# Where a decoder trunk forms the query and key weights of its attention units 8, 9 and 10

## The chip, the cores and the metric

The kernel runs on one core of one Trainium2 chip, in one launch. The metric is the device time of an execution in microseconds; less is better. Times are medians of several runs.

## The reference

The reference is a decoder trunk of two layers over 1024 positions of width 1024, all in 32-bit floats. Each layer has a token mixer and then a dense MLP with a squared ReLU; each of these is preceded by an RMS norm and added to the residual, and a final RMS norm ends the trunk.

```python
for layer in range(DEPTH):                      # DEPTH = 2
    y = _rms_norm(h, mix_norm_g[layer])
    if layer % 2 == 0: y = _chunk_gating_mixer(y, ...)      # spatial gating MLP, chunks of 128
    else:              y = _dilated_attention_mixer(y, w_qkv, w_out, rel_bias)
    h = h + y
    y = _rms_norm(h, mlp_norm_g[layer])
    h = h + jnp.square(jax.nn.relu(y @ w_up[layer])) @ w_down[layer]
return _rms_norm(h, final_norm_g)
```

The mixer of layer 0 is a gating MLP. That of layer 1 is a causal attention with 8 heads of 64 in each of three dilation groups (1, 4 and 16), whose outputs are merged by their softmax denominators. The MLPs go from 1024 to 4096 and back.

## The kernel before, in words

**Numbers.** TensorE multiplies in a reduced format (fp32r). To keep the accuracy of 32-bit floats, each operand is split into an upper and a lower half (hi and lo), and a product is three matmuls: hi by hi, hi by lo, lo by hi. Function `split` (L219 to L221) does this: ScalarE copies the source to hi (L220), and an engine, mostly VectorE, subtracts hi from the source to give lo (L221). Nearly all tiles are 128 by 512.

**Products by seven.** The large products are formed by a scheme of Strassen's kind: of a 2 by 2 block product, seven products (numbered 1 to 7) of sums and differences of blocks are computed instead of eight. So each weight comes as four blocks, from which seven operands are formed by a few additions and seven splits.

**Order of the phases.** Gating mixer of layer 0, up and down projection of the first MLP, values of the attention, the attention's 12 units, output projection, and the second MLP. A unit is a pair of heads in one dilation group; `unit_qk` computes its queries and keys with seven products from the weights `wd[i, p]` of unit `i`. Scores, softmax, transposes and products with the values of earlier units are woven between these products by a planner (`Flow`), which counts TensorE's time while the program is written and lets generators go on when their due time has come. The order of TensorE is thereby fixed in the program; the order of the other engines follows the program and the dependencies, each engine's queue being in order.

**Weights formed ahead.** The seven operands of a unit's weights are formed ahead of time and saved in DRAM (`wd`): loaded blocks are added, subtracted, split, and hi and lo are stored. In the attention they are only loaded again (`unit_weights`, tile wp, L1241), seven loads of 512 KB for a unit. Before the change they are formed in these places:
- units 1 to 6 in the gating mixer, by `prepare`;
- unit 11 (`APART`) in the up projection of the first MLP, by `prepare_apart`, after other weights;
- unit 7 among the values of the attention, by `attended`;
- units 8, 9 and 10 in the attention itself, by `attended` with a pace of 7000 ns a part, from 12 us after the first unit's start on.

`prepare_apart(i)` is a generator of eight parts for a unit. All eight together issue 6 loads of 256 KB, 4 additions or subtractions on VectorE (L584 to L600) and 7 splits. `placed` puts the 14 stores of the halves on a list (`unsaved`), and `save` issues what is on the list on SP's queue (L556); it is called after a later step, so that a store doesn't wait for its split at the head of the queue. The attention's version keeps its tiles apart from the others: loaded blocks and lower halves in the ring r (4 tiles, name ra), upper halves in the ring b (2 tiles, name hi), which the attention's bias tiles use as well. The other places take all tiles from the ring t (13 tiles, names t and tr).

**The down projection** (`Down.run`) has 18 steps, `t` = 0 to 17. A step forms one block column of the output with seven products of up to four k-blocks, in the order 1, 5, 7, 6, 2, 3, 4; with four k-blocks a product has 12 matmuls. After each product, VectorE empties the bank into h (L1067) or into a sum (L1099); after product 1, ScalarE copies it. Behind that, for each product, `then` calls `more()`, which forms one of the seven weights wp of the next step (GpSimd makes the sums, L376 to L381, ScalarE and VectorE split), and `inputs`, which loads one hidden tile (t from hid) and splits it into hx for the next step. Banks `d` and `e` hold products 5 and 7 and, emptied, products 3 and 4. In the last steps fewer k-blocks are left, the products are shorter, and the last inputs (xe) are loaded. Then `close` ends the layer and the first tiles of the attention begin.

Of the kernel before, what the change touches and what calls it, by code (L numbers as in the profile page):

```python
# [12 lines left out]
F32 = mybir.dt.float32  # L13
F32R = mybir.dt.float32r
# [5 lines left out]
P = 128  # L20
D = 1024
S = 1024
HALF = 512
# [8 lines left out]
def half(s):  # L32
    return slice(s * HALF, (s + 1) * HALF)


def blk(b, n=1):
    return slice(b * P, (b + n) * P)
# [75 lines left out]
LATER = (2, 4, 6)  # L113

CALM = (1600.0, 1600.0, 1200.0, 1600.0)
PREPARED = ((1, 2, 3, 4, 5, 6), (7,), (8, 9, 10))
APART = 11
EARLY = 4
PACE = (1700.0, 1800.0, 3000.0, 7000.0)
LAT = dict(sum=2600.0, rms=2600.0, tile=1600.0, gate=8500.0, soft=5500.0, turn=4200.0, fe=1300.0, v=2000.0, qk=4200.0, merge=2600.0, out=700.0, fex=3.0, ve=1600.0, vd=6000.0, ex=18000.0, ones=900.0)  # L120


# [1 line left out]
def trunk(ctx: ExitStack, tc: tile.TileContext, xT, w_u, w_v, w_o, w_s, b_s, w_qkv, w_vt, w_bo, rel,  # L124
          w_up, w_dn, w_dl, vecs, onehot, outT):
    nc = tc.nc
    flow = Flow()
# [4 lines left out]
    tpool = ctx.enter_context(tc.tile_pool(name="tpool", bufs=13))  # L132
# [3 lines left out]
    dram = ctx.enter_context(tc.tile_pool(name="dram", bufs=2, space=DRAM))  # L136
# [8 lines left out]
    def rtemp():  # L145
        return tpool.tile([P, HALF], F32R, tag="t", name="tr")
# [5 lines left out]
    class Pair:  # L152
# [6 lines left out]
        def split(self, src, engine=None):  # L159
            n = src.shape[1]  # L160
            split(self.hi[:, 0:n], self.lo[:, 0:n], src, engine)
            return self
# [13 lines left out]
    def load(src, t=None):  # L176

        src, n = src if isinstance(src, list) else [src], 0
        t = raw() if t is None else t
        for x in src:  # L180
            nc.sync.dma_start(t[:, n:n + x.shape[1]], x)
            n += x.shape[1]
        return t[:, 0:n]

    def mm_bank():
        return psm.tile([P, HALF], F32, tag="mm", name="mm")
# [157 lines left out]
    SEVEN = (1, 5, 7, 6, 2, 3, 4)  # L344
# [155 lines left out]
        flow.add((terms.second if s else terms.first)(sq, gi), LAT["sum"])  # L500


    wd = {(i, p): dram.tile([P, 2, HALF], F32, name=f"wd{i}_{p}", bufs=1) for i in (*sum(PREPARED, ()), APART) for p in SEVEN}

    def prepare(unit_list, pace):

# [32 lines left out]
    LATE_DL = {("dl", 1, a): w_dl[1, a] for a in range(4)}  # L539
    wl = {key: dram.tile([P, 2, HALF], F32, name="wl" + "_".join(map(str, key)), bufs=1) for key in (*LATE, *LATE_DL)}  # L540

    def fetch(src, own=rtemp):
        r = own()
        return r, load(src, r.bitcast(F32))

    def apart():
        return tpool.tile([P, HALF], F32R, tag="r", name="ra", bufs=4)

    def above():
        return tpool.tile([P, HALF], F32R, tag="b", name="hi", bufs=2)  # L550

    unsaved = []

    def save():
        for dst, t in unsaved:
            nc.sync.dma_start(dst, t.bitcast(F32))  # L556
        unsaved.clear()

    def placed(dst, held, own=rtemp):
        lo, r = held  # L560
        hi = own()
        split(hi, lo, r)
        unsaved.extend((dst[:, e, :], t) for e, t in enumerate((hi, lo)))

    def prepare_late(src):

        keys = list(src)
        held = fetch(src[keys[0]])
        yield
        for n, key in enumerate(keys):  # L570
            last, held = held, fetch(src[keys[n + 1]]) if n + 1 < len(keys) else None
            placed(wl[key], last)
            yield

    def prepare_apart(i, own=rtemp, upper=rtemp):

        tt = nc.vector.tensor_tensor
        n = 3 * (i // 3 * 3 + ORDER[i % 3])
        src = lambda a, b: w_qkv[n + a][:, half(b)]
        get = lambda a, b: fetch(src(a, b), own)  # L580
        put = lambda p, held: placed(wd[i, p], held, upper)
        r10, r11 = get(1, 0), get(1, 1)
        yield
        tt(r10[1], r10[1], r11[1], op=ALU.add)  # L584
        r00 = get(0, 0)
        put(4, r11)
        yield
        x = own()
        x = x, x.bitcast(F32)
        tt(x[1], r10[1], r00[1], op=ALU.subtract)  # L590
        put(5, r10)
        yield
        r11 = get(1, 1)
        put(1, r00)
        yield
        tt(r11[1], r11[1], x[1], op=ALU.subtract)
        r01 = get(0, 1)
        put(7, r11)
        yield
        tt(r01[1], r01[1], x[1], op=ALU.subtract)  # L600
        again = get(0, 1)
        put(3, r01)
        yield
        put(6, x)
        yield
        put(2, again)
        yield

    def attended(unit_list, pace, *own):
        for i in unit_list:  # L610
            for _ in prepare_apart(i, *own):
                yield pace
                save()
        save()

    coming_late = [chain(prepare_late(LATE), prepare_apart(APART)), prepare_late(LATE_DL)]

    def late(*key, place=None):
        w = (place or wpair)()
        nc.sync.dma_start(w.t.bitcast(F32), wl[key])  # L620
        return w
# [106 lines left out]
    for gi, chunks in enumerate(((0, 1, 2), (3, 4, 5), (6, 7))):  # L728
        banks = {}
        for k in range(KT):  # L730
# [29 lines left out]
            for e, i, n, f in order:  # L760
                x, c = ys[n // 4][k], blk(n % 4)
# [31 lines left out]
    for tiles in ((0, 1, 2), (3,), (4,), (5, 6, 7)):  # L793
        w = [weight(w_u[m]) for m in tiles]
        if tiles[0] == 3:
            flow.add(prepare(PREPARED[0], PACE[0]))
        for s in range(2):
            for i, m in enumerate(tiles):
                b = mm_bank()
# [9 lines left out]
    for tiles in ((0, 1), (2,), (3,), (4, 5, 6, 7)):  # L809
        w = [weight(w_o[m]) for m in tiles]  # L810
        for s in range(2):
            for i, m in enumerate(tiles):
                b = mm_bank()
# [196 lines left out]
    class Down:  # L1010
# [43 lines left out]
        def run(self, w):  # L1054
            for t, (a, ks) in enumerate(self.todo):
                hs = {(i, s): h[a + 4 * i][:, half(s)] for i in range(2) for s in range(2)}
                wn = None
                if t < 17:
                    wn = self.weights(t + 1, **(dict(own=temp, place=pair) if t == 16 else {}))
                more = ahead(wn)  # L1060
                more()

                def xs(p):
                    return [self.x[self.order[k]][p] for k in ks]

                def add(i, s, src, engine=nc.vector):
                    return engine.tensor_tensor(hs[i, s], hs[i, s], src, op=ALU.add).ins  # L1067

                def then(evacuated, p):

                    with tc.issue_after(evacuated) if t < 3 else nullcontext():
                        more()
                        self.inputs(t + 1, (p,))

                if t == 16:
                    self.ends(0)
                a_ = mm_bank()
                product(a_, w[1], xs(1))
                if t < 4:
                    self.u[a] = spare() if t < 2 else temp()  # L1080
                    more()
                    nc.scalar.activation(self.u[a], a_, AF.Copy)
                    self.inputs(t + 1, (1,))
                else:
                    more()
                    sums = mm_bank()
                    nc.scalar.activation(sums, a_, AF.Copy)
                    self.inputs(t + 1, (1,))
                d = at_bank()
                product(d, w[5], xs(5))  # L1090
                then(add(1, 1, d), 5)
                e = at_bank()
                product(e, w[7], xs(7))
                then(add(1, 1, e), 7)
                if t == 16:
                    self.ends(1)
                b = at_bank() if t < 4 else sums
                product(b, w[6], xs(6), t >= 4)
                then(nc.vector.tensor_tensor(self.u[a], self.u[a], b, op=ALU.add).ins, 6)  # L1099
                product(a_, w[2], xs(2), True)  # L1100
                then(add(0, 0, a_), 2)
                product(d, w[3], xs(3), True)
                then(add(0, 1, d), 3)
                if t >= 14:
                    for i, s in ((1, 1), (0, 1)):
                        add(i, s, self.u[a], nc.gpsimd)
                product(e, w[4], xs(4), True)
                self.emptied = add(1, 0, e)
                then(self.emptied, 4)
                if t >= 14:  # L1110
                    add(1, 0, self.u[a], nc.gpsimd)
                w = wn
# [96 lines left out]
    def own(t, g):  # L1209
        return t if g == 0 else t.rearrange("p (q r) -> p q r", r=DIL[g])  # L1210
# [71 lines left out]
    def value_operands():  # L1282
# [3 lines left out]
        fetched = lambda p, k: [load(w_vt[a, b + k], raw() if p == 5 and not b else temp()) for a, b in parts[p]]  # L1286
        total, held = {}, [fetched(*x) for x in order[:EARLY]]
        for n, (p, k) in enumerate(order):
            r = held.pop(0)
            if n + EARLY < len(order):  # L1290
                held.append(fetched(*order[n + EARLY]))
            x = r[0]
# [10 lines left out]
    def all_values():  # L1303

        operands, wv = value_operands(), []
        for s in range(2):
# [13 lines left out]
            for b, bank in enumerate(banks):  # L1320
                value_store(0, 4 * s + b, bank)
        flow.add(terms_a.differences(PACE[1]))

# [8 lines left out]
        for n, p in enumerate(VSEQ):  # L1332
# [6 lines left out]
            if p == 6:  # L1339
                flow.add(attended(PREPARED[1], PACE[2]))  # L1340
            opens = p in (1, 2, 5)
# [440 lines left out]
    all_values()  # L1782
    for gen in (scorer, turner, valuer):
        flow.add(gen())
    flow.add(attended(PREPARED[2], PACE[3], apart, above), 12000.0)
    for i in range(NU):
        unit_qk(i)
    sq = [Square(half(s), (0, 5)) for s in range(2)]
# [127 lines left out]
```

## Time and profile before

| | |
|---|---|
| runs without profile, us | 2141.2, 2147.09, 2149.47 (median 2147.09) |
| profiled execution, us | 2150.69 |
| its span, first to last instruction, us | 2149.0 |
| TensorE busy (matmuls) | 2103.0 us, 98% |
| VectorE busy | 1575.6 us, 73% |
| ScalarE busy | 1183.9 us, 55% |
| GpSimd busy | 498.0 us, 23% |
| mean granted TensorE clock | 0.993 |

In the profile's rows, PE is TensorE (PEld its weight loads), DVE is VectorE, ACT is ScalarE, POOL is GpSimd and SP the engine that issues nearly all DMAs; a q behind a name is the engine's sequencer, L192 a line of the kernel, and out<-in are tiles by their names in the program. Matmuls are pipelined, so that the recorded duration of one is longer than the distance to the next. A row of waits names who waited, the releaser, the total in us, the number of waits and the longest. The chain of waits is followed back from the last instruction to what released it at each point. All window times are us from the start of the span. Weights of units 8 to 10 are formed from 1059.7 to 1281 us of the profiled execution; the steps 6 to 18 of the first down projection lie between 686 and 905 us.

### The profile page before, as it was taken

The page shows a single profiled execution, that of the slowest core. Times are in us where ns is not written, and L with a number is a line of the kernel's source. Part 1 is how long each engine was busy: PE and PEld are TensorE (multiplying, and loading weights), DVE is VectorE, ACT ScalarE, POOL GpSimd, SP SyncE. Part 2 cuts the span into 40 slices and gives each one's busy share as a digit, 9 for nine tenths or more (in the row PEclk, how much of TensorE's full clock was granted, in tenths as well). Part 3 has the DMA queues.
Part 4 walks back from the last instruction along what each step waited for, and adds up shares of the span by engine and source line. Part 5 has one row for each costly group of instructions (what it writes and reads, how often), then busy time and mean ns, then how long its engine had stood idle before and what let it go on. Part 6 is the DMA issues. An engine that isn't in the chain of part 4 may idle for free.

```text
span 2149.0 us, 30646 instructions
## 1 busy us (share of the span) xinstructions
PE 2103.0 (98%) x10144; PEld 1736.4 (81%) x10144; DVE 1575.6 (73%) x2904; ACT 1183.9 (55%) x2384; POOL 498.0 (23%) x370
## 2 busy tenths in 40 slices
PE   8999999999999999999998989999999999999997
PEld 7888888888878888878887778877888888888886
DVE  7878769666689777787666666656985555988776
ACT  7645436566665444346466665666465556544432
POOL 2000224332333332420000000002442332432244
PEclk9999999999999999999999999999999999999998
DMA  6338814587765453445876766481256443654432
GB/s 216 123 92 285 289 55 151 199 274 276 261 202 188 154 160 118 160 174 200 316 217 217 227 202 182 154 266 59 79 201 210 153 157 123 211 162 153 147 113 79
DMA packets 224756, 387.10 MB, mean 180 GB/s; under 512 B 39897, under 2 KB 67668, under 8 KB 224596
## 3 DMA queue, kind: packets, MB, share of 16 engines
q1 hardware_dynamic: 215456, 383.77, 53.8%
q10 hardware_dynamic: 9140, 1.36, 0.4%
q8 instruction: 80, 1.31, 0.3%
q14 instruction: 80, 0.66, 0.1%
HBM read 252.24 MB, written 132.81 MB: 179 GB/s over the span
## 4 chain that ended last, share of the span: by engine, by line
PE 79%; DVE 8%; DMA 6%; ACT 3%; issue 2%; POOL 1%; SPq 1%; ACTq 0%; DVEq 0%; POOLq 0%
PE at L192 40%; PE mm L192 39%; DMA wd<-hi 2%; PE at L199 1%; DMA t<-in_w_qkv 1%; DVE tr L221 1%; DVE t L221 1%; DVE y L221 1%; POOL t L278 1%; DMA r<-in_w_v 1%; ACT t L1496 1%; DVE wp L221 1%; DMA V<-vd 0%; DVE r L438 0%; DVE h L333 0%
## 5 line engine op out<-in xcount | busy, mean ns | idle before, releaser
L221 DVE TENSOR_TENSOR wp<-r,wp 128x512 fp32r<-128x512 f32 (+3 forms) x399 | 322.8, 814 | 138.9 <-ACT wp L220 136.5
L220 ACT ACTIVATE wp<-r 128x512 fp32r<-128x512 f32 (+3 forms) x399 | 236.0, 596 | 328.4 <-PE at L192 202.5
L192 PE MATMUL mm<-t,wp 128*128 128x512 f32 x1368 | 348.7, 398 | 1.1 <-DVE k L1420 0.6
L192 PE MATMUL at<-hx,wp 128*128 128x512 f32 x1452 | 340.9, 389 | 1.8 <-DVE h L1067 1.8
L192 PEld LDWEIGHTS at<-hx,wp 128*128 128x128 f32 x1452 | 272.3, 188 | 59.8 <-DVE h L1067 2.6
L192 PEld LDWEIGHTS mm<-t,wp 128*128 128x128 f32 x1368 | 251.8, 189 | 55.5 <-DVE k L1420 1.7
L278 POOL TENSOR_TENSOR t<-t 128x512 f32<-128x512 f32 (+1 forms) x64 | 82.2, 1284 | 837.9 <-ACT t L273 835.8
L192 PE MATMUL at<-y,wp 128*128 128x512 f32 x1008 | 245.3, 389 | 0.0
L192 PE MATMUL mm<-hx,wp 128*128 128x512 f32 x984 | 234.2, 389 | 0.0
L192 PEld LDWEIGHTS at<-y,wp 128*128 128x128 f32 x1008 | 189.1, 188 | 39.6 <-issue 0.4
L192 PEld LDWEIGHTS mm<-hx,wp 128*128 128x128 f32 x984 | 184.6, 188 | 38.5 <-DVE hx L221 0.3
L192 PE MATMUL mm<-y,wp 128*128 128x512 f32 x816 | 210.9, 397 | 1.1 <-DVE y L221 0.6
L376 POOL TENSOR_TENSOR t<-r 128x512 f32<-128x512 f32 (+3 forms) x62 | 83.7, 1350 | 478.9 <-DMA r<-in_w_up 137.3
L192 PEld LDWEIGHTS mm<-y,wp 128*128 128x128 f32 x816 | 149.7, 189 | 33.1 <-DVE y L221 1.0
L221 DVE TENSOR_TENSOR hx<-t,hx 128x512 fp32r<-128x512 f32 x192 | 162.1, 849 | 7.9 <-ACT hx L220 7.9
L192 PE MATMUL mm<-y,whi 128*128 128x512 f32 x512 | 158.2, 390 | 0.0
L192 PE MATMUL at<-t,wp 128*128 128x512 f32 x552 | 130.6, 389 | 0.0
L220 ACT ACTIVATE hx<-t 128x512 fp32r<-128x512 f32 x192 | 118.8, 627 | 20.3 <-DMA t<-hid 11.6
L378 POOL TENSOR_TENSOR r<-r 128x512 f32<-128x512 f32 (+3 forms) x62 | 90.5, 1459 | 163.5 <-DVE wp L221 159.8
L1067 DVE TENSOR_TENSOR h<-h,at 128x512 f32<-128x512 f32 x144 | 97.9, 680 | 35.9 <-PE at L192 35.4
L192 PEld LDWEIGHTS at<-t,wp 128*128 128x128 f32 x552 | 103.6, 188 | 21.5
L192 PEld LDWEIGHTS mm<-y,whi 128*128 128x128 f32 x512 | 95.6, 188 | 19.5
(250 smaller groups left out, 3483.7 us busy)
## 6 DMA issues: line engine op xcount, KB each, us to landing
t<-hid SPq DMA_DIRECT2D x182, 256.0 KB, 4.2
wp<-wd SPq DMA_DIRECT2D x77, 512.0 KB, 5.2
hid<-t SPq DMA_DIRECT2D x140, 256.0 KB, 2.9
r<-in_w_up SPq DMA_DIRECT2D x120, 256.0 KB, 2.8
wd<-tr SPq DMA_DIRECT2D x112, 256.0 KB, 2.9
r<-in_w_dn SPq DMA_DIRECT2D x80, 256.0 KB, 2.6
hid<-b SPq DMA_DIRECT2D x56, 256.0 KB, 2.9
r<-in_w_v SPq DMA_DIRECT2D x48, 256.0 KB, 3.0
```

Of the source, the lines that this page charges most:

```text
L192: nc.tensor.matmul(out, lhsT, rhs, **kw)
L199: nc.tensor.transpose(out, src, ident)
L220: nc.scalar.activation(hi, src, AF.Copy)
L221: (engine or nc.vector).tensor_tensor(lo, src, hi.bitcast(F32), op=ALU.subtract)
L278: nc.gpsimd.tensor_tensor(self.acc, self.acc, sq, op=ALU.add)
L376: tt(r3, r[0, 0], r[1, 0], op=ALU.subtract)
L378: tt(r[1, 1], r[1, 0], r[0, 0], op=ALU.subtract)
L1067: return engine.tensor_tensor(hs[i, s], hs[i, s], src, op=ALU.add).ins
L1496: nc.scalar.activation(p[:, c], p[:, c], AF.Exp, bias=m, scale=-1.0, accum_out=dn)
```

## The change

The weights of units 8, 9 and 10 are no longer formed in the attention. A generator `beside` runs through the 24 parts of the three units, and the down projection of the first MLP calls it twice a step, behind products 5 and 3 (`STEPS`), in the steps `t` = 5 to 17. Ahead of each part, `save` stores what the part before has split. All tiles are now from the ring t, and the separate tiles in the rings r and b are no longer used for this.

```diff
-PREPARED = ((1, 2, 3, 4, 5, 6), (7,), (8, 9, 10))
+PREPARED = ((1, 2, 3, 4, 5, 6), (7,))
 APART = 11
+BESIDE = (8, 9, 10)
+STEPS = (5, 3)
...
-PACE = (1700.0, 1800.0, 3000.0, 7000.0)
+PACE = (1700.0, 1800.0, 3000.0)
...
-    def fetch(src, own=rtemp):
-        r = own()
+    def fetch(src):
+        r = rtemp()
         return r, load(src, r.bitcast(F32))
-
-    def apart():
-        return tpool.tile([P, HALF], F32R, tag="r", name="ra", bufs=4)
-
-    def above():
-        return tpool.tile([P, HALF], F32R, tag="b", name="hi", bufs=2)
...
     coming_late = [chain(prepare_late(LATE), prepare_apart(APART)), prepare_late(LATE_DL)]
+    beside = chain(*(prepare_apart(i) for i in BESIDE))
...
                     with tc.issue_after(evacuated) if t < 3 else nullcontext():
                         more()
                         self.inputs(t + 1, (p,))
+                    if self.layer == 0 and t >= 5 and p in STEPS:
+                        save()
+                        next(beside, None)
...
-    flow.add(attended(PREPARED[2], PACE[3], apart, above), 12000.0)
     for i in range(NU):
         unit_qk(i)
```

More of the change, by code (lines that the diff above doesn't have):

```diff
@@ L500, in start_terms @@
         flow.add((terms.second if s else terms.first)(sq, gi), LAT["sum"])
-    wd = {(i, p): dram.tile([P, 2, HALF], F32, name=f"wd{i}_{p}", bufs=1) for i in (*sum(PREPARED, ()), APART) for p in SEVEN}
+    wd = {(i, p): dram.tile([P, 2, HALF], F32, name=f"wd{i}_{p}", bufs=1) for i in (*sum(PREPARED, BESIDE), APART) for p in SEVEN}
     def prepare(unit_list, pace):
@@ L557, in save, with placed @@
         unsaved.clear()
-    def placed(dst, held, own=rtemp):
+    def placed(dst, held):
         lo, r = held
-        hi = own()
+        hi = rtemp()
         split(hi, lo, r)
@@ L573, in prepare_late, with prepare_apart @@
             yield
-    def prepare_apart(i, own=rtemp, upper=rtemp):
-        tt = nc.vector.tensor_tensor
+    def prepare_apart(i, tt=nc.vector.tensor_tensor):
         n = 3 * (i // 3 * 3 + ORDER[i % 3])
         src = lambda a, b: w_qkv[n + a][:, half(b)]
-        get = lambda a, b: fetch(src(a, b), own)
-        put = lambda p, held: placed(wd[i, p], held, upper)
+        get = lambda a, b: fetch(src(a, b))
+        put = lambda p, held: placed(wd[i, p], held)
         r10, r11 = get(1, 0), get(1, 1)
@@ L587, in prepare_apart @@
         yield
-        x = own()
+        x = rtemp()
         x = x, x.bitcast(F32)
@@ L607, in prepare_apart, with attended @@
         yield
-    def attended(unit_list, pace, *own):
+    def attended(unit_list, pace):
         for i in unit_list:
-            for _ in prepare_apart(i, *own):
+            for _ in prepare_apart(i):
                 yield pace
```

## Prediction

> **What bounds the kernel now.** I read the page's slices first, then the busy time by stage, then the waits and the chain of the two stages that the change touches. A 0.5% difference (10.7 us) is about the least that a measurement of this kernel can tell from no change.
>
> ```profile
> PE   8999999999999999999998989999999999999997
> ```
>
> TensorE is busy in nearly every slice, so the rest of the machine counts only where it makes TensorE late. The slices that dip in the middle are the attention. The table by stage (window and its length, then each engine's busy us and instruction count, granted clock, DMA share, GB/s) separates three kinds of time:
>
> ```profile
> core 0: us, PE busy (x) PEld busy (x) DVE busy (x) ACT busy (x) POOL busy (x), PEclk, DMA share, GB/s
> 1060.00:1123.00 63.00, 63.00 (x374) 51.46 (x373) 36.37 (x110) 39.00 (x106) 0.00 (x0) 1.00 0.76 238
> 1123.00:1298.00 175.00, 160.20 (x959) 129.81 (x959) 117.46 (x362) 108.17 (x298) 0.00 (x0) 0.96 0.68 212
> 1298.00:1409.00 111.00, 109.71 (x695) 90.87 (x695) 77.83 (x235) 72.61 (x199) 0.00 (x0) 1.00 0.55 166
> 712.00:731.00 19.00, 19.00 (x85) 15.77 (x84) 15.61 (x21) 9.23 (x15) 5.90 (x4) 1.00 0.48 154
> 731.00:750.00 19.00, 19.00 (x85) 15.73 (x84) 14.93 (x21) 9.22 (x15) 5.97 (x4) 1.00 0.46 152
> 686.00:838.00 152.00, 152.00 (x672) 125.91 (x671) 121.70 (x161) 73.11 (x120) 46.42 (x33) 1.00 0.47 152
> 838.00:906.00 68.00, 68.00 (x301) 56.33 (x300) 48.20 (x71) 24.17 (x47) 29.50 (x26) 1.00 0.40 136
> ```
>
> Attention from 1123 to 1298 leaves TensorE idle for 14.8 us, with the clock at 0.96; from 1298 to 1409, the same kind of work leaves 1.3 us idle at full clock. The down projection of the first MLP, from its sixth step (686 us) to its end (905 us), has no idle TensorE time at all, but VectorE is busy for 15.6 and 14.9 us in two windows of 19.0 us.
>
> Who makes TensorE and ScalarE wait from 1123 to 1298 (total us, times, longest), and the chain of waits from 1060 to 1298 (start, us, what):
>
> ```profile
> PE at L192 <- DVE N L1535: 7.4, 5, 2.5
> PE at L192 <- DVE tr L221: 3.6, 5, 1.7
> ACT hi L220 <- DMA wd<-hi: 12.0, 5, 3.4
> DVE b L1197 <- DMA wd<-hi: 5.7, 2, 3.4
> ...
> by line: PE mm L192 29.7%; DMA wd<-hi 15.4%; PE at L192 10.4%; ACT t L1496 5.1%; issue 4.0%; PE at L199 3.8%; ACT hi L220 3.5%; DVE tr L221 3.0%; DVE q L1420 2.9%; DMA wd<-ra 2.8%; DMA ex<-sc 2.7%; DVE N L1535 2.3%; ACT q L1419 2.0%; ACT N
> 1127.54 5.51 DMA wd<-hi
> 1203.78 5.16 DMA wd<-hi
> 1236.67 5.45 DMA wd<-hi
> ```
>
> The direct releasers of TensorE are small VectorE results of the attention itself, but behind them stands a store. The upper half of a prepared weight (hi) lives in a ring of two tiles, shared with the bias tiles b. ScalarE's next hi copy stands at the head of its queue until the store of an earlier hi has landed, 12.0 us in five waits, and the attention's copies and exponentials queue behind it; VectorE's bias copy (L1197) does the same for 5.7 us. The stores wd<-hi and wd<-ra make 18.2% of this stretch's chain.
>
> **The change part by part.** What leaves the attention, and what the same instructions cost there (min/median/max ns, first and last start in us):
>
> ```profile
> L220 ACT ACTIVATE hi<-ra x21: 613/632/642, 1093.1 to 1279.6; 128x512 fp32r<-128x512 f32 x21
> L221 DVE TENSOR_TENSOR ra<-ra,hi x21: 640/691/694, 1093.7 to 1280.2; 128x512 fp32r<-128x512 f32 x21
> L556 SPq DMA_DIRECT2D wd<-ra x21: 319/319/395, 1094.5 to 1281.0; - x21
> L181 SPq DMA_DIRECT2D ra<-in_w_qkv x18: 332/383/458, 1059.7 to 1247.0; - x18
> L584 DVE TENSOR_TENSOR ra<-ra x3: 689/692/693, 1067.7 to 1214.5; 128x512 f32<-128x512 f32 x3
> ```
>
> For three units that is 21 ScalarE copies (13.3 us), 21 VectorE subtractions and 12 sums or differences (four groups like L584; 33 x 0.69 = 22.8 us), 18 loads and 42 stores on SP. The last store starts at 1281, and the idle TensorE time ends at 1298, so the two stretches differ by just this work.
>
> *Attention.* Work is compared by matmul count, which needs the same mix of sizes. The wide matmuls of each stretch, 1123 to 1298 first:
>
> ```profile
> L192 PE MATMUL mm<-t,wp 128*128 128x512 f32 x235 | 67.1, 419 | 1.1 <-DVE k L1420 0.6 <-ACT t L1430 0.5
> L192 PE MATMUL mm<-y,wp 128*128 128x512 f32 x168 | 46.1, 407 | 0.0
> ...
> L192 PE MATMUL mm<-t,wp 128*128 128x512 f32 x162 | 43.7, 405 | 0.0
> L192 PE MATMUL mm<-y,wp 128*128 128x512 f32 x131 | 35.7, 404 | 0.0
> ```
>
> They are 403 of 959 and 293 of 695, 42% in both. The clean stretch needs 111.0 / 695 = 0.160 us for a matmul; 959 of them would take 153.2 us instead of 175.0. So 21.8 us are to be had: the idle time, and slow matmuls while the clock is down. The lower bound takes the idle time alone, less the clean stretch's rate of it: 14.8 - 1.3 x 175 / 111 = 12.8 us. I take 21.8, because the wide matmuls of the first stretch are longer too (419 against 405 ns), which only the clock explains, and the clock falls after idle stretches. There is nothing to gain before 1123, where TensorE is never idle. A loss in the attention is excluded, since nothing is added there.
>
> *Down projection, steps 6 to 13 or so.* The 24 parts of the three units come at two places of each step, behind the second and the sixth of its seven products. That is 33 VectorE instructions over 12 steps, 2.75 a step. At 0.69 us they take 1.9 us of the 3.4 to 4.1 us in which VectorE now idles per step. But VectorE there works beside GpSimd (5.9 us a step), which is idle in the attention, and the like subtraction beside it shows a price of its own:
>
> ```profile
> L221 DVE TENSOR_TENSOR hx<-t,hx x192: 674/680/1832, 595.4 to 2054.2; 128x512 fp32r<-128x512 f32 x192
> ```
>
> So each may take from 0.69 to 1.83 us; the two ends give 1.9 and 5.0 us a step, and the second doesn't fit into 4.1 us. I take a value near the first, since the median is 0.68. The Trainium skill, "SBUF — State Buffer", Who interferes with whom, speaks against this move: a VectorE instruction with two SBUF inputs and a reading GpSimd instruction exclude one another for a whole instruction. By that rule alone every moved instruction that meets GpSimd takes the longer time; the row's maximum agrees, its median shows that most meet none.
>
> What hides the delay is PSUM: a bank is filled by one product and reopened four products later, so its VectorE reading has three products between, and a product takes 19.04 / 7 = 2.72 us (rows of the chain from 838 to 906, start and us; the first two are the starts of two steps):
>
> ```profile
> 852.69 2.72 PE mm L192 x12
> 871.73 2.04 PE mm L192 x9
> 886.01 1.36 PE mm L192 x6
> 892.81 2.72 PE at L192 x12
> ```
>
> That is 8.2 us against a delay of 1.4 us (two instructions) or 3.7 us (two at 1.83). No TensorE time is lost: 0.
>
> SP has its own queue. It is not full, but its loads run little ahead:
>
> ```profile
> 712.49 5.27 SPq L181 DMA_DIRECT2D r<-in_w_dn  x3
> 717.80 1.86 SPq L181 DMA_DIRECT2D t<-hid  x4
> ...
> 731.52 5.28 SPq L181 DMA_DIRECT2D r<-in_w_dn  x3
> ...
> t<-hid SPq DMA_DIRECT2D x182, 256.0 KB, 4.2
> ```
>
> The first row holds three loads over 5.3 us of waiting for buffers; the hidden tiles behind them land in 4.2 us. The change adds 60 DMAs, 5 a step, 1.6 to 2.3 us of issue (0.32 for a store, up to 0.46 for a load above), and their tiles come from the same ring of 13 (t) as the hidden tiles. Behind a store that waits stand the next hidden loads; behind these ScalarE's copies hx, and behind VectorE's half of hx the emptying of the banks. The inputs are made a whole step (19 us) ahead, so a few us pass unseen. I take 0 here, with a bound of the rivals' price.
>
> *Last steps.* From 871.73 the products shorten to 2.04 us, then from 886.01 to 1.36 us, and the cover shrinks to 4.1 us. VectorE runs without a gap there:
>
> ```profile
> 885.67 0.67 DVE L1067 TENSOR_TENSOR h<-h,at 128x512 f32<-128x512 f32 x1
> 888.30 0.67 DVE L1067 TENSOR_TENSOR h<-h,at 128x512 f32<-128x512 f32 x1
> 891.01 1.47 DVE L1067 TENSOR_TENSOR h<-h,at 128x512 f32<-128x512 f32 x2
> ```
>
> The first of the two additions at 891.01 is done at 891.7, and its bank is reopened at 892.81: 1.1 us are left. The two parts in the step from 871.73 hold four VectorE instructions (a difference and a subtraction each), 2.8 us, of which about 1 us falls into gaps; 1.8 - 1.1 = 0.7 us is the least. At 1.83 us each it is 7.3 - 1.0 - 1.1 = 5.2 us. I take 1.5, nearer to the first, as GpSimd is busy there for less than half of the window (29.5 of 68 us).
>
> *Sum.* -21.8 + 0 + 1.5 = -20.3 us. The profiled execution took 2150.69 us (span 2149.0 and 1.7 around it), so its like would take 2130.4; it lies 3.6 us above the median of the timed runs, 2147.09, from which the forecast is 2126.8, rounded **2127**.
>
> **The rivals.**
>
> *Half the gain.* TensorE's own waits name N, tr and st, parts of the attention that stay. If half the idle time is theirs, the gain is 10.9 - 1.5 = 9.4 us: 2137.7. For it: those names, and a load ex<-sc in the chain. Against it: the clean stretch has the same instructions, and hardly an idle us.
>
> *VectorE meets GpSimd each time.* A step then asks of VectorE 15.3 (mean of the two windows) + 5.0 + 1.1 for the waits on ScalarE between a copy and its subtraction (1.75 splits at 0.63) = 21.4 us against 19.04. Twelve steps lose 28.3 us, the sum is +6.5: 2153.6. [...]
>
> *VectorE becomes the bound of the down projection and waits for loads too.* In the attention the prepared tiles had rings of their own; here their loads share a ring and SP's order with the hidden tiles. In before, tile ra was waited for like this:
>
> ```profile
>   DMA ra<-in_w_qkv: 4.8, 4
> ```
>
> One such wait (1.2 us) in each step, on top of the former rival, makes 22.6 us a step, 3.6 too many, 42.7 in twelve: +20.9, 2168. It decides as soon as VectorE's step, waits included, is over 19.04 us; below that it costs nothing. For it: a shared ring of 13 in which the three units hold four to six tiles. Against it: 3.4 to 4.1 us of idle VectorE a step, and inputs a step ahead.
>
> That the weights aren't formed at all is excluded: 13 steps from the sixth on have 26 places for 24 parts, and the 25th saves the last.
>
> **How the numbers follow.** Forecast 0.69, half the gain 0.14, GpSimd each time 0.05, VectorE and loads 0.12. The range starts at the whole 21.8 without cost, 2125.3, less 4 for the spread of three runs (2141.2 to 2149.47), 2121; it ends at the half gain with the same 4, 2142. The last two cases, 0.17, stay outside. Faster by over 0.5% (below 2136.4) is the forecast and the better third of the half gain, 0.74; within 0.5% are the rest of that and the GpSimd case, 0.14; slower is the last, 0.12.
>
> **What would show it.** Right: no wd store between 1040 and 1300, the chain there without wd, TensorE idle under 3 us and a granted clock of 1.00 in the stretch of 959 matmuls, which lasts about 153 us; VectorE 17 to 18 of 19 us in the steps of the down projection, TensorE still without gaps until about 890, and 1 to 2 us lost there. Wrong: TensorE waiting at L192 for h L1067 or hx within the steps, SP waiting long before the loads of hid, or an attention that keeps its idle time.

## The result, and the profile after

The change makes the kernel faster: 2124.32 us (median of 6 runs, 2122.41 to 2126.35) against 2147.34 us of before, a ratio of 0.9892 (95% interval 0.9875 to 0.9909), or 23 us. The forecast was 2127 in a range of 2121 to 2142. The profiled execution took 2122.84 us, 27.9 us less than that of before.

TensorE's slices of the page after (line numbers are two higher than before at the helpers, so matmuls are now L194, splits L222 and L223):

```profile
PE   9999999999999999999999999999999999999997
```

The dip in the attention is gone. The table by stage, with the attention's window set to about the same work as in the prediction (columns as there):

```profile
1123.00:1276.00 153.00, 152.36 (x972) 126.10 (x971) 102.50 (x336) 100.31 (x281) 0.00 (x0) 1.00 0.55 163
712.00:731.00 19.00, 19.00 (x85) 15.73 (x85) 17.28 (x24) 10.13 (x18) 6.20 (x4) 1.00 0.59 196
731.00:750.00 19.00, 19.00 (x86) 15.74 (x85) 17.48 (x24) 10.12 (x18) 6.27 (x4) 1.00 0.79 256
686.00:838.00 152.00, 152.00 (x672) 125.96 (x671) 140.41 (x186) 79.97 (x134) 47.90 (x33) 1.00 0.67 222
838.00:906.00 68.00, 67.32 (x294) 54.53 (x293) 54.08 (x79) 26.25 (x52) 30.48 (x26) 1.00 0.61 207
```

The first row held 959 matmuls in 175 us before; now there are 972 in 153 us, at full clock, with 0.6 us idle. The down projection's full steps still have no idle TensorE time, though VectorE went from 15.6 and 14.9 to 17.3 and 17.5 us of 19.0. The last row lost 0.7 us of TensorE's busy time.

How long the attention takes can be read from one row of each kernel: the first and the last start of the copy q, the first result of a unit (12 units). Before, and after:

```profile
L1419 ACT ACTIVATE q<-mm x12: 576/1084/1117, 1062.1 to 1423.9; 128x512 fp32r<-128x512 f32 x12
L1418 ACT ACTIVATE q<-mm x12: 574/1082/1105, 1061.7 to 1399.1; 128x512 fp32r<-128x512 f32 x12
```

That is 361.8 us and 337.4 us, so 24.4 us of the profiled execution's 27.9 are the attention's. The rest is 0.4 us ahead of it (the down projection's third step ends 2.0 us earlier, with the same code ahead of it, and its last steps lose 1.8, below), and 3.1 us behind it; the time from the last q to the end lies between 721.7 and 725.3 us in all the kernels run here but the one with other lags, with the same code there, so that nothing is read into it. The chain of waits from 1060 to 1298, where stores made 18%, is now:

```profile
by line: PE mm L194 67.2%; PE at L194 22.4%; PE at L201 9.2%; DVE t L1666 0.8%; DVE tr L223 0.6%; issue 0.0%
```

TensorE itself makes 98.8% of it; no DMA is left in it.

### The profile page after: what moved, and what is told of

It reads as the page before. It is cut to its first block, busy times and chain, and to the rows that moved or that the text cites. A ratio compares the mean times of both kernels' runs of the same rounds, so it can differ in the third digit from the quotient of the medians.

```text
span 2121.1 us, 30688 instructions
## 1 busy us (share of the span) xinstructions
PE 2093.4 (99%) x10144; PEld 1731.3 (82%) x10144; DVE 1581.4 (75%) x2904; ACT 1182.4 (56%) x2384; POOL 498.7 (24%) x370
## 4 chain that ended last, share of the span: by engine, by line
PE 86%; DVE 7%; DMA 4%; issue 1%; ACT 1%; POOL 1%; SPq 0%; POOLq 0%; DVEq 0%; ACTq 0%
PE mm L194 43%; PE at L194 40%; PE at L201 2%; DVE y L223 1%; DVE t L223 1%; DMA r<-in_w_v 1%; DMA t<-in_w_qkv 1%; DVE wp L223 1%; DMA V<-vd 0%; DVE r L440 0%; DVE hx L223 0%; DVE tr L223 0%; POOL t L280 0%; DMA t<-hid_(1, 0)_6229 0%; DVE h L1063 0%
## 5 line engine op out<-in xcount | busy, mean ns | idle before, releaser
L223 DVE TENSOR_TENSOR wp<-r,wp 128x512 fp32r<-128x512 f32 (+3 forms) x399 | 321.0, 810 | 128.8 <-ACT wp L222 126.9
L222 ACT ACTIVATE wp<-r 128x512 fp32r<-128x512 f32 (+3 forms) x399 | 236.0, 597 | 321.5 <-PE at L194 199.5
L194 PE MATMUL mm<-t,wp 128*128 128x512 f32 x1368 | 345.5, 396 | 0.5 <-DVE t L985 0.5
L194 PE MATMUL at<-hx,wp 128*128 128x512 f32 x1452 | 341.1, 390 | 1.7 <-DVE h L1063 1.6
L194 PEld LDWEIGHTS at<-hx,wp 128*128 128x128 f32 x1452 | 272.3, 188 | 59.9 <-DVE h L1063 3.2
L194 PEld LDWEIGHTS mm<-t,wp 128*128 128x128 f32 x1368 | 250.7, 188 | 53.3 <-DVE t L985 0.9
L194 PE MATMUL at<-y,wp 128*128 128x512 f32 x1008 | 245.3, 389 | 0.0
L194 PE MATMUL mm<-hx,wp 128*128 128x512 f32 x984 | 234.2, 389 | 0.3 <-ACT mm L1086 0.3
L194 PEld LDWEIGHTS at<-y,wp 128*128 128x128 f32 x1008 | 189.1, 188 | 39.5 <-issue 0.4
L194 PEld LDWEIGHTS mm<-hx,wp 128*128 128x128 f32 x984 | 184.7, 188 | 38.9 <-ACT mm L1086 0.7
L194 PE MATMUL mm<-y,wp 128*128 128x512 f32 x816 | 210.5, 397 | 1.2 <-DVE y L223 0.6
L194 PEld LDWEIGHTS mm<-y,wp 128*128 128x128 f32 x816 | 149.1, 188 | 33.3 <-DVE y L223 1.1
L223 DVE TENSOR_TENSOR hx<-t,hx 128x512 fp32r<-128x512 f32 x192 | 165.2, 865 | 5.9 <-ACT hx L222 5.9
L194 PE MATMUL mm<-y,whi 128*128 128x512 f32 x512 | 158.4, 390 | 0.0
L194 PE MATMUL at<-t,wp 128*128 128x512 f32 x552 | 130.6, 389 | 0.0
L222 ACT ACTIVATE hx<-t 128x512 fp32r<-128x512 f32 x192 | 119.0, 627 | 19.2 <-DMA t<-hid 15.2
L194 PEld LDWEIGHTS at<-t,wp 128*128 128x128 f32 x552 | 103.6, 188 | 21.5
L194 PEld LDWEIGHTS mm<-y,whi 128*128 128x128 f32 x512 | 95.6, 188 | 19.5
```

What stands on the lines that cost most here:

```text
L194: nc.tensor.matmul(out, lhsT, rhs, **kw)
L222: nc.scalar.activation(hi, src, AF.Copy)
L223: (engine or nc.vector).tensor_tensor(lo, src, hi.bitcast(F32), op=ALU.subtract)
```

## The experiments

Eleven kernels were run. Three ask what in the forming of weights held the attention up, three split its engine work, and one moves the planner's lags; one asks what the forming costs in the down projection, and three shift it there. A twelfth, e12, has no time: it was the kernel before with all tiles of units 8 to 10 from the ring t of 13, and its program comes to a deadlock. Kernels with an e-number from e2 on, e8 and e12 aside, start from the kernel after. The code is shown shortened. Ratios are to before on the same chip; the kernel after stands at 0.9892.

**e1: upper halves from the large ring.** Before, with

```diff
-    flow.add(attended(PREPARED[2], PACE[3], apart, above), 12000.0)
+    flow.add(attended(PREPARED[2], PACE[3], apart), 12000.0)
```

> The kernel before, with one thing changed: the upper halves of units 8 to 10 in the attention come from the ring t of 13 tiles instead of the ring b of two; loads, sums, splits, stores and their places stay. Theory ring (a copy stands at ScalarE's head until the store of an earlier hi has landed, and the attention queues behind it): the 12 us of waits of hi on wd vanish, TensorE's idle time in the prepared stretch (1123 to 1298 in before, 14.8 us) falls below 5 us, and the time falls by 13 to 20 us, to 2128 to 2135. Rival work (54 more instructions on VectorE and ScalarE are what the attention can't hide): nothing of them is gone, time 2143 to 2150 and 12 us idle or more. Rival traffic (60 more DMAs slow the loads the attention waits for): the same 2143 to 2150.

Measured: 0.9994 (0.9981 to 1.0007), and an attention of 1062.2 to 1429.2, 367.0 us. Its waits from 1060 to 1300:

```profile
DVE ra L596 <- DMA ra<-in_w_qkv: 11.3, 2, 9.0
PE mm L192 <- DVE k L1420: 10.5, 3, 8.0
ACT q L1419 <- DMA sc<-st: 9.2, 1, 9.2
DVE ra L590 <- DMA wd<-ra: 7.6, 1, 7.6
```

The wait that the prediction blamed, ScalarE's hi on wd<-hi, is gone, and nothing is won. VectorE now stands 11.3 us before a load and 7.6 us before a store of the other ring, that of four tiles (ra), and TensorE waits 8.0 us at once for a result behind the latter. (ScalarE's row of 9.2 us is at the same place: its copy q reads a sum that VectorE ended at 1137.84 us, behind the wait of 7.6, and q starts at 1137.87.) The two small rings take each other's place, so the ring of two was not the cause by itself.

**e2: engine work and loads, no stores.** After, and in the attention the same parts once more without saving:

```diff
+    def again(unit_list, pace):     # the parts of prepare_apart in the rings r (4) and b (2), no stores
+        ...
+    flow.add(again(BESIDE, 7000.0), 12000.0)
     for i in range(NU):
```

> The kernel after, and beside it the whole engine work and the 18 loads of forming units 8 to 10 once more in the attention, in the old places and the old rings of four and two tiles, but without the 42 stores (its results are not used). Theory ring: a hi tile is free as soon as its subtraction is done, so nothing stands at ScalarE's head; 0 to 5 us over the kernel after, 2124 to 2130, TensorE's idle time in the attention's units up to 1400 us below 5 us. Rival work: back to the time of before, 2143 to 2150. Rival traffic: a third of its loss, from the 18 loads, about 2131.

Measured: 0.9935 (0.9915 to 0.9954). **e5: the same work on resident tiles**, without loads in its course, **e6: its VectorE part alone**, **e7: its ScalarE part alone**:

```diff
+    a, b = apart(), apart()                          # loaded once
+    ...
+    tt(c, a, b, op=ALU.add)                          # e5, e6: 12
+    nc.scalar.activation(hi, a, AF.Copy)             # e5, e7: 21
+    tt(apart(), a, hi, op=ALU.subtract)              # e5, e6: 21 (e6: b for hi)
```

> The kernel after, and in the attention in the old places the engine work of forming the three units once more (12 sums and 21 subtractions on VectorE, 21 copies on ScalarE, in the old rings) on two tiles that are loaded once, so without loads and stores in the course of it; its results are not used. In the run with loads and without stores the attention from the first unit to the last took 16.0 us more than after. Theory work (instructions in order on VectorE and ScalarE lengthen the attention's own chains): about the same, 10 to 16 us, ratio to before 0.993 to 0.997. Theory loads (what stands at the head of a queue is an instruction that waits for its load): 0 to 4 us, ratio 0.989 to 0.991.

> As the run with resident tiles, but only the 33 VectorE instructions, no copies on ScalarE. If VectorE's share carries the loss, 8 to 14 us over after in the attention; if the loss needs both (a subtraction that stands waiting for its copy, a copy that stands before an exponential), under 4 us.

> As the run with resident tiles, but only the 21 ScalarE copies. If ScalarE's share carries the loss, 6 to 12 us over after in the attention; if the loss needs both engines, under 3 us.

Measured: 0.9936 (0.9921 to 0.9951), 0.9910 (0.9888 to 0.9932) and 0.9884 (0.9867 to 0.9902). The row of q in e2, e5, e6 and e7, in this order:

```profile
L1463 ACT ACTIVATE q<-mm x12: 570/1084/1105, 1063.8 to 1417.2; 128x512 fp32r<-128x512 f32 x12
L1441 ACT ACTIVATE q<-mm x12: 574/1084/1108, 1065.8 to 1415.4; 128x512 fp32r<-128x512 f32 x12
L1441 ACT ACTIVATE q<-mm x12: 575/1086/1108, 1063.7 to 1407.8; 128x512 fp32r<-128x512 f32 x12
L1441 ACT ACTIVATE q<-mm x12: 573/1085/1107, 1063.6 to 1402.5; 128x512 fp32r<-128x512 f32 x12
```

The attention takes 16.0, 12.2, 6.7 and 1.5 us more than after. So instructions that wait for no DMA in their course account for about half of the 24.4 us, as the theory of work expected for e5. The copies of ScalarE alone, which run from 1094.6 to 1254.9 us in e7, much as before (1093.1 to 1279.6), are thus not the cause. VectorE's share stays open, because e6 did not put its instructions in the old places. The 21 subtractions of e5, then those of e6:

```profile
L631 DVE TENSOR_TENSOR ra<-ra,hi x21: 670/684/702, 1097.4 to 1266.7; 128x512 fp32r<-128x512 f32 x21
L631 DVE TENSOR_TENSOR ra<-ra x21: 670/679/706, 1069.9 to 1102.0; 128x512 fp32r<-128x512 f32 x21
```

With no copy to follow, all 33 VectorE instructions of e6 run between 1069.3 and 1102.0 us, and its 6.7 us are the price of that burst. In e5 TensorE waits for the attention's own small results, with no tile of the weights among the releasers:

```profile
PE at L194 <- DVE N L1557: 2.9, 2, 1.5
PE mm L194 <- DVE k L1442: 1.5, 2, 1.1
```

Loads add 3.8 us by these rows, and the stores the last 8.4 (24.4 - 16.0). By the medians, engine work is 0.0044 of the time of before (9 us), loads nothing that can be told, and the stores 0.0065 (14 us). The profiled e2 took 2144.09 us against a median of 2137.93, so the shares are no finer than that: engine work 9 to 12 us, the DMAs and the waits on them 12 to 14. Nor are they parts of the same waits: from the first q of the third unit to that of the fourth it is 36.0 us before, 29.3 after, 30.2 in e2 and 29.5 in e5, but from there to the fifth 38.5, 35.9, 38.7 and 41.4.

**e3: the DMAs without the work.** After, and in the attention 18 loads, and 42 stores from a tile that stays:

```diff
+                for _ in range(loads):  load(w_qkv[n][:, half(0)])
+                for _ in range(stores): nc.sync.dma_start(next(scratch), kept_tile)
```

> The kernel after, and in the attention in the old places the 18 loads of 256 KB and 42 stores of 256 KB on SP's queue, with no work on ScalarE or VectorE (all stores read one tile that stays, and write scratch memory). Theory ring: no engine waits for a store, 0 to 4 us over the kernel after, 2124 to 2129. Rival work: the same. Rival traffic: most of the 21.8 us come back, 2140 to 2148, with longer waits for V, ex or wp.

Measured: 0.9921 (0.9903 to 0.9939), attention 1061.9 to 1411.3, 349.4 us, 12.0 more than after. This is between the two expectations. The DMAs did not keep to the old places: with no work to wait for, the stores go out from 1068.6 to 1158.0 us, where those of before took from 1093.7 to 1281.0. One event makes the 12.0 us (SP's rows at that place, then ScalarE's):

```profile
1125.07 0.67 SPq L1254 DMA_DIRECT2D wp<-wd  x1
1125.78 1.28 SPq L183 DMA_DIRECT2D r<-in_w_qkv  x2
1127.63 2.89 SPq L622 DMA_DIRECT2D scratch<-r  x4
1130.63 0.42 SPq L1397 DMA_DIRECT2D V<-vd  x1
1132.53 1.28 ACTq L1622 DMA_DIRECT2D sc<-st  x2
1133.85 0.63 ACT L1432 ACTIVATE q<-t 128x512 fp32r<-128x512 f32 x1 [11.64 <-DMA r<-in_w_qkv]
```

ScalarE issues a small transfer of its own there, in two DMAs (the exchange of row maxima, sc<-st). It did nothing from 1122.2 on (1133.85 less 11.64), and the first of the two went out only at 1132.53; the attention's copy q stood behind it for 11.6 us. The trace shows what it waited for. In this program the DMAs of all queues count their landings on eight semaphores, taken in turn, and where the trace tells the landing, no DMA goes out before the last one on its semaphore, as a rule the eighth ahead of it, has landed (694 cases in after, 725 in e3). Here these were two loads of SP that sc<-st has nothing to do with: wp<-wd of 1125.07, landed at 1132.45, and for the second DMA the first r<-in_w_qkv of 1125.78, landed at 1133.16. All other units take as long as after. The traffic itself is thus hidden, though denser than in before; it cost only where it got to the head of an engine's queue.

**e8: longer lags of the planner**, before with

```diff
-soft=5500.0, turn=4200.0, ... qk=4200.0
+soft=7000.0, turn=5700.0, ... qk=5700.0
```

> The kernel before, with three lags of the planner 1.5 us longer (scores to transposes 7.0, transposes to products with the values 5.7, queries and keys to scores 5.7 us), so that TensorE's fixed order asks for the results of VectorE and ScalarE later. Theory work: the idle time of 14.8 us in the stretch 1123 to 1298 comes from results that are 0.6 to 3 us later than planned, and half of it or more goes: ratio to before 0.992 to 0.997. Theory stores (waits of 3 to 8 us on DMAs at the head of a queue): little changes, 0.997 to 1.003, since the lag is longer than 1.5 us.

Measured: 1.0294 (1.0273 to 1.0316), slower, which neither theory had. TensorE's longest wait is then another:

```profile
PE at L192 <- DMA V<-vd: 28.9, 9, 5.6
```

The likely reason is that with later products the values' tiles are free later, and their loads come late. The experiment says nothing on the question it was made for.

**e4: units 8 to 10 not formed at all.** They load the weights of units 5 to 7.

> The kernel after without forming units 8 to 10 anywhere; these units load the formed weights of units 5 to 7 instead, seven loads as before. It measures what the 24 parts cost in the down projection. By the prediction's sum they cost 1.5 us (0.7 to 5.2), all of it in the steps from the sixteenth on: 2120 to 2124, with no difference in the steps 6 to 15. If the down projection hides less than that (VectorE bound), the time falls further, below 2117.

Measured: 0.9878 (0.9860 to 0.9896), which overlaps with the kernel after; in the profile the attention takes 337.6 us (1060.7 to 1398.3), as after. So in after the attention has nothing left of the forming, and its price in the down projection shows in the chain alone. The rows are the last two products of the down projection's third step, the first product of its fourteenth and of its sixteenth, and the last product of all, in before, after and e4 (start us, us):

```profile
643.62 4.39 PE at L192 x18
838.41 2.04 PE mm L192 x9
871.73 2.04 PE mm L192 x9
902.33 2.73 PE at L192 x12
```
```profile
641.62 4.40 PE at L194 x18
836.42 2.04 PE mm L194 x9
869.74 2.04 PE mm L194 x9
902.14 2.73 PE at L194 x12
```
```profile
642.26 4.37 PE at L194 x18
837.03 2.04 PE mm L194 x9
870.35 2.04 PE mm L194 x9
900.95 2.73 PE at L194 x12
```

The fourteenth step starts 194.79, 194.80 and 194.77 us behind the first of these rows: the parts cost nothing up to there. From the start of the sixteenth to the end of the last product it is 33.3, 35.1 and 33.3 us: the change costs 1.8 us, all in the last three steps.

**e9, e10, e11: other places in the down projection.** After, with `t >= 3` instead of `t >= 5` (e9), or with other `STEPS`:

```diff
-STEPS = (5, 3)
+STEPS = (5, 6, 3)              # e10
+STEPS = (5, 7, 6, 2, 3, 4)     # e11
```

> The kernel after with the parts beside the steps from the fourth on instead of the sixth, so that the 24 parts end with the fifteenth step and none lies in the three short ones. Theory last steps (the 1.8 us that the kernel after loses between the start of the first full step and the end of the last step are lost from the sixteenth step on): they come back, 2120 to 2123 on the scale of the kernel after, ratio to before 0.987 to 0.989. Rival: the fourth and fifth step have no VectorE time to spare (43.0 us busy of 43.0 between 643 and 686 us in before), and four parts there cost 2 to 6 us: ratio 0.989 to 0.992.

> The kernel after with three parts beside each step, behind the products 5, 6 and 3, so that all are formed in the steps 6 to 13. VectorE then needs 15.3 + 4.1 x 0.77 (what an instruction added per step in the kernel after: 2.1 us for 2.75) = 18.4 of 19.04 us a step. Theory bound at 19.04: no loss in these steps, and the 1.8 us of the last steps come back: ratio 0.987 to 0.989. If VectorE's order already hurts below its full load: over 2 us are lost in the steps 6 to 13.

> The kernel after with a part behind each of six products of a step, so that all are formed in the steps 6 to 9. VectorE then needs 15.3 + 8.25 x 0.77 = 21.6 us of 19.04 a step, 2.6 us too many in each of four, 10 us in all, of which the cover of three products (8.2 us) can hold a part. Theory bound at 19.04: TensorE waits for VectorE's additions in these steps, 2 to 8 us, and the 1.8 us of the last steps come back: ratio 0.988 to 0.993. If the load doesn't decide: 0 lost, ratio 0.987 to 0.989.

Measured: 0.9885 (0.9867 to 0.9902), 0.9880 (0.9861 to 0.9899) and 0.9940 (0.9922 to 0.9957). In e10 the same two landmarks are

```profile
642.77 4.40 PE at L194 x18
901.48 2.73 PE at L194 x12
```

so 261.44 us from the start of the first to the end of the second, as in before (261.44; after has 263.25): nothing is lost, neither in the full steps nor in the last ones, with VectorE at 17.9 to 18.9 of 19 us in five windows, this one the fullest:

```profile
743.00:762.00 19.00, 19.00 (x86) 15.73 (x85) 18.89 (x26) 10.14 (x18) 6.18 (x5) 1.00 0.82 267
```

This is what the theory of a bound at 19.04 us expected. e9 has half of both of its cases: nothing is lost in the last steps, but TensorE waits 1.9 us in the fifth, where the chain runs through a late load of a hidden tile (a row of the waits, one of the chain):

```profile
PE mm L194 <- ACT mm L1086: 1.9, 1, 1.9
670.88 3.34 DMA t<-hid
```

By the chain e10 is the best version of those run, but by its times it can't be told from the kernel after.

e11 is 0.0048 over after, 10 us, more than the 2 to 8 us expected, and shows what an overfull step does. TensorE waits for ScalarE's copy into a bank, and ScalarE for loads of hidden tiles (waits from 686 to 785, then the first and the last of the windows of 19 us in which TensorE waits):

```profile
ACT hx L222 <- DMA t<-hid: 23.6, 15, 4.3
PE mm L194 <- ACT mm L1086: 7.2, 3, 3.6
705.00:724.00 19.00, 16.58 (x66) 13.22 (x65) 18.91 (x25) 10.28 (x19) 6.54 (x4) 0.91 0.91 314
762.00:781.00 19.00, 15.25 (x65) 11.73 (x65) 16.56 (x27) 8.92 (x17) 1.31 (x1) 1.00 0.84 273
```

VectorE is full in the first of these windows (18.9 of 19 us) and not in the last (16.6). The two limits hang together: in the chain, a subtraction of a part on VectorE (773.25 us) holds up the store of its result at the head of SP's queue (773.88), and the load of a hidden tile goes out behind that (774.24). Which of them gives out first the run doesn't tell. The prediction's rival of a full VectorE that also waits for loads is this; it holds with six parts a step, and with neither two nor three.

## Why the prediction was right, point by point

*Size of the attention's gain.* 21.8 us for the stretch from 1123 to 1298, and 0 before it. After, 972 matmuls take 153.0 us, so 959 take 151.0 instead of the 153.2 worked out. That makes 24.0 us, and over all units the gain is 24.4. Comparing a disturbed stretch with a clean one of the same mix by matmul count was right to about a tenth, the clean rate (0.160 us a matmul) being a little slower than that of this stretch (0.157); the lower bound from idle time alone, 12.8, would have been half.

*Its cause.* This step was wrong in part. It read a chain with 18% of stores and 12.0 us of waits of hi on wd, and concluded that the ring of two held the attention up. e1 took that wait away and won nothing. Half of the loss is plain work on VectorE and ScalarE in their order (e5), the other half is tied to the DMAs, mostly the stores (e2), by whichever small ring or queue comes first (e1). That stores are waited for in turn by each ring is read from e1's waits and not shown otherwise, since e12, with the large ring for all tiles, gave no time. The eight semaphores of the DMAs (e3), through which 60 DMAs more had to pass, are another candidate that no run tried by itself. It made no difference to the forecast because the change moved all of it; of a change to the ring alone, this step would have promised a gain that e1 didn't have.

*Half the gain.* That rival gave TensorE's direct releasers N and tr to the attention itself, to stay. They went: 0.6 us of idle time remain in the stretch of 153 us.

*Steps 6 to 15.* 0 was right, to 0.01 us. VectorE rose by 2.1 us in the mean of the two windows, and by 18.7 us from 686 to 838. The parts' own 23 instructions of that stretch (the first row below, tile tr alone: VectorE's busy time is the third) took more, 23.86 us or 1.04 each, about a third of the way from 0.69 to 1.83; for the instructions themselves, a value near the first was low. (By busy time, the 0.77 of e10 and e11 fits: the five windows of e10 have 18.4 us in the mean.)

```profile
686.00:838.00 152.00, 0.00 (x0) 0.00 (x0) 23.86 (x23) 8.62 (x14) 1.00 0.67 222
690.35 1.62 POOL L383 TENSOR_TENSOR r<-r 128x512 f32<-128x512 f32 x1 [1.29 <-DMA tr<-in_w_qkv]
690.75 1.78 DVE L223 TENSOR_TENSOR tr<-tr 128x512 fp32r<-128x512 f32 x1
```

Eight of the 23 took 1.6 to 1.8 us, and each of these began while a GpSimd instruction ran, as in the last two rows. The Trainium skill, "SBUF — State Buffer", Who interferes with whom, says that a VectorE instruction with two SBUF inputs contends with a GpSimd instruction that reads SBUF; the trace agrees for single instructions. But the other 15 took 0.7 us, and the rival in which each meets GpSimd fell.

*Last steps.* 1.5 us forecast, 1.8 measured, and in the steps it named. The mechanism was another, though. It wasn't mainly the number of VectorE instructions, but SP's queue, which runs late with the parts' transfers in it (rows after, then before; the step starts at 869.74 and at 871.73 us):

```profile
874.74 0.47 SPq L183 DMA_DIRECT2D t<-hid_(1, 0)_6229  x1
875.30 3.92 SPq L552 DMA_DIRECT2D wd<-tr  x2
881.62 0.32 SPq L183 DMA_DIRECT2D t<-hid_(0, 1)_6231  x1
883.55 0.32 SPq L183 DMA_DIRECT2D t<-hid_(1, 1)_6233  x1
893.55 1.62 SPq L183 DMA_DIRECT2D r<-in_w_vt  x3
897.93 0.63 ACT L222 ACTIVATE wp<-r 128x512 fp32r<-128x512 f32 x1 [7.20 <-DMA r<-in_w_vt]
```
```profile
873.45 0.43 SPq L181 DMA_DIRECT2D t<-hid_(1, 0)_6229  x1
877.24 9.79 SPq L181 DMA_DIRECT2D r<-in_w_vt  x4
```

The chain after goes through two late loads. An input, t<-hid_(1, 0), goes out 5.0 us behind the start of the step instead of 1.7, and takes 8.11 us to land; VectorE idles 1.24 us for xe and does its subtractions and additions late. Later, three of the four loads in_w_vt go out from 893.55 us on, where before had issued all four by 887; ScalarE stands 7.20 us before the first of them, and the copy that empties a bank is behind that. Two stores of a part also stand in front of the next two inputs, which go out at 881.6 and 883.6 us instead of 873.9 and 874.4, but the chain doesn't pass there. The prediction had looked at SP only for the full steps, where it took 0. That the parts in these steps are the cause is shown by e9 and e10, which have none there and lose nothing; how much of the 1.8 us each late load costs isn't shown.

## What to carry to other kernels

The worth of moving work out of a stage can be read by comparing it with a clean stretch of the same mix, instruction for instruction; TensorE's idle time alone gave half of it. A long wait in the chain names a place where time was lost, not the thing whose removal wins it back: where an engine's order is full of foreign work, taking one wait away lets the next one come forward. Background work goes where every consumer has a step's lead, and in the steps that run out of lead, look at the loads that its transfers will make late. And before the time of an experiment is read, its trace has to show that the instructions run where they were meant to: those of e6 and the DMAs of e3 had moved forward.

## What was not expected of the hardware

A DMA that ScalarE itself issues can hold ScalarE up: in e3 the issue of sc<-st went out some 10 us late, when an unrelated load of SP on the same semaphore had landed. VectorE can be filled to 18.9 of 19 us beside a busy TensorE without costing it anything (e10), while with six parts a step TensorE lost 2.4 us of a window with VectorE at 18.9, and 3.75 us of one with VectorE at 16.6, where hidden tiles came late (e11).
